# Loads whose source runs span several partitions: 48 KB reads for 12 KB and 24 KB destination rows

## The chip, the cores and the metric

One core of a Trainium2 chip, the others idle. The metric is device time in microseconds of one execution. The rounds of the experiments ran on three chips (0, 12 and 3 in the record), each with the kernel before beside them; hence its medians of 261.81, 262.06 and 262.07 us. "Ratio" is the mean time of one kernel's fast runs over that of the kernel before in the same rounds, with a 95% interval, so it is not quite the ratio of the medians that stand beside it.

## The reference

```python
batch, m, k, n = 16, 512, 768, 1024
x: (batch, k, m) float32;  y: (batch, k, n) float32
out = np.einsum('bkm,bkn->bmn', x, y)          # float32, (16, 512, 1024)
```

Per batch 1.57 MB of x and 3.15 MB of y come in, 2.10 MB go out: 109.05 MB in all.

## The kernel before

K is laid over the 128 partitions with six neighbouring k rows each, so that one partition's share of x is one run of 12 KB in HBM (the device memory) and that of y one of 24 KB. The loads go into float32 staging tiles (two of each), are cast to bfloat16 on the vector engine (DVE), multiplied, copied from PSUM (where matmul results arrive) by the scalar engine, and stored four batches late. All transfers are issued by the sync engine (SP) on one queue.

```python
x_v = x.rearrange("b (p ko) m -> b p ko m", ko=KT)      # KT = 6
y_v = y.rearrange("b (p ko) n -> b p ko n", ko=KT)
o_v = out.rearrange("b (p mo) n -> b p mo n", mo=MT)    # MT = 4
...
for b in range(B):
    xs = xs_pool.tile([P, KT, M], FP32, name="xs")      # bufs=2
    ys = ys_pool.tile([P, KT, N], FP32, name="ys")      # bufs=2
    nc.sync.dma_start(xs[:], x_v[b])
    nc.sync.dma_start(ys[:], y_v[b])
    if b >= LAG:                                        # LAG = 4
        store(b - LAG)
    ...
    nc.vector.tensor_copy(x_sb[:], xs[:])
    for h in range(2):
        ks = slice(h * KT // 2, (h + 1) * KT // 2)
        nc.vector.tensor_copy(y_sb[:, ks], ys[:, ks])
    ...   # 48 matmuls, 8 evictions
for b in sorted(o_tiles):
    store(b)
```

## Time and profile before

| | before |
|---|---|
| median time | 261.97 us (261.96 to 262.15, 3 runs) |
| span in the profile | 260.1 us |
| busiest compute engine | PE 74% |
| packets in flight on the load and store queue | 98.5% of 16 engines' span |
| period of two batches | 31.63 us |

Read it as follows. A busy share of 74% is no bound; the queue's share is. The two staging buffers make the chain repeat every two batches, so the distance between a y cast and the one two batches later is the pace of the steady state. I take it throughout as the mean of the four last periods, from the y cast of batch 7 to that of batch 15: (235.12 - 108.59) / 4 = 31.63 us. From the chain in order of time (start, duration, what):

```profile
108.59 3.44 DVE y_sb L65 x2
...
235.12 1.76 DVE y_sb L65
```

### The profile page before, as it was taken

To read this page: it belongs to the slowest core of one execution; us is meant where nothing else is said; L and a number is where in the kernel's file an instruction comes from. 1 tells how busy PE (TensorE), PEld (TensorE's weight loads), DVE (VectorE), ACT (ScalarE), POOL (GpSimd) and SP (SyncE) were. 2 spreads that over 40 slices of the span, in tenths; PEclk is the share of its full clock that TensorE was granted. 3 is DMA by queue.
4 is the path that set the end of the run, shared out by engine and by line. 5 is a ranking of instruction groups with operands and counts; after the bars stand their busy time and mean duration, and the time that the engine had idled before them with its cause. 6 is when DMAs were issued, how large, how long until landed. Compare 5 with 4: busy or idle time off the path is not lost.

```text
span 260.1 us, 1877 instructions
## 1 busy us (share of the span) xinstructions
PE 192.3 (74%) x768; PEld 89.3 (34%) x768; DVE 83.0 (32%) x48; ACT 76.4 (29%) x129; POOL 0.2 (0%) x4
## 2 busy tenths in 40 slices
PE   0059999896947939599597886939779395895950
PEld 0014555353523514235143342514334142351420
DVE  0271643525213252222524215252132522225000
ACT  1003444342421403314123241413324042141330
POOL 0000000000000000000000000000000000000000
PEclk9999999999997998959779797997999899796895
DMA  7999999999999999999999999999999999999995
GB/s 299 427 423 420 438 433 427 431 369 422 430 430 432 432 430 435 430 432 423 433 435 421 438 422 438 429 427 437 435 424 424 432 431 430 437 425 432 431 408 242
DMA packets 6921, 109.18 MB, mean 420 GB/s; under 512 B 768, under 2 KB 768, under 8 KB 768
## 3 DMA queue, kind: packets, MB, share of 16 engines
q1 hardware_dynamic: 6912, 109.05, 98.5%
q8 instruction: 6, 0.10, 0.1%
q14 instruction: 3, 0.02, 0.0%
HBM read 75.50 MB, written 33.55 MB: 419 GB/s over the span
## 4 chain that ended last, share of the span: by engine, by line
DMA 80%; DVE 10%; PE 5%; DVEq 1%; SPq 0%; issue 0%; ACT 0%
DMA ys<-in_y_dram 80%; DVE y_sb L65 10%; PE ps L74 5%; DVEq L106 1%; SPq L56 0%; ACT o_sb L76 0%; SPq L57 0%; DVEq L65 0%
## 5 line engine op out<-in xcount | busy, mean ns | idle before, releaser
L74 PE MATMUL ps<-y_sb,x_sb 128*128 128x512 bf16 x768 | 192.3, 413 | 58.4 <-DVE y_sb L65 58.4
L74 PEld LDWEIGHTS <-x_sb 128*128 128x128 bf16 x768 | 89.3, 118 | 160.9 <-issue 47.5
L76 ACT COPY o_sb<-ps 128x512 f32<-128x512 f32 x128 | 75.2, 587 | 174.1 <-PE ps L74 174.1
L65 DVE CAST y_sb<-ys 128x3072 bf16<-128x3072 f32 x32 | 54.9, 1757 | 89.4 <-DMA ys<-in_y_dram 89.4
L62 DVE CAST x_sb<-xs 128x3072 bf16<-128x3072 f32 x16 | 28.2, 1760 | 66.2 <-DMA xs<-in_x_dram 55.2
L76 ACT ACT_TABLE_LOAD x1 | 1.3, 1283 | 0.7 <-PEq L95 0.7
L95 POOL MEMSET const-uint8-127<- 128x1 uint8 x1 | 0.1, 103 | 0.0
L95 POOL MEMSET const-bfloat16-1.0<- 128x1 bf16 x1 | 0.1, 102 | 0.0
L95 POOL MEMSET const-float32-1.0<- 128x1 f32 x1 | 0.1, 100 | 0.0
L95 POOL MEMSET const-float32-0.0<- 128x1 f32 x1 | 0.1, 99 | 0.2 <-issue 0.2
## 6 DMA issues: line engine op xcount, KB each, us to landing
ys<-in_y_dram SPq DMA_DIRECT2D x16, 3072.0 KB, 28.1
out_dram<-o_sb SPq DMA_DIRECT2D x16, 2048.0 KB, 32.6
xs<-in_x_dram SPq DMA_DIRECT2D x16, 1536.0 KB, 29.7
```

Source lines behind the costliest of these rows:

```text
L62: nc.vector.tensor_copy(x_sb[:], xs[:])
L65: nc.vector.tensor_copy(y_sb[:, ks], ys[:, ks])
L74: nc.tensor.matmul(ps[:], x_w[:, kt, mo], y_sb[:, kt, ns], start=(kt == 0), stop=(kt == KT - 1))
L76: nc.scalar.copy(o_sb[:, mo, ns], ps[:])
L95: nc = _bacc.Bacc("TRN2", target_bir_lowering=False, num_devices=1)
L106: with _tile.TileContext(nc) as tc:
```

## The change

The intent, from the packet records that the prediction reads: a transfer shows 144 packets (6912 for 48 transfers), and their median times leave about 8 ns a packet at zero bytes. If one read covers four partitions' rows of x, or two of y, there are fewer reads, of 48 KB. The destination keeps one row per partition, 12 KB of x and 24 KB of y.

```diff
+    def load(dst, src, rows):
+        like = template.ins
+        pat = mybir.BassSymbolicTensorAccessPattern
         ...
+        wide = src.rearrange("(q r) k m -> q (r k m)", r=rows)
+        flat = dst.rearrange("p k m -> p (k m)")
+        nc.sync.add_instruction(_copy.replace(
+            like, name=nc.get_next_instruction_name(),
+            ins=(pat(ap=wide.ap, dtype=wide.dtype, bass_ap=wide, **copy_args),),
+            outs=(pat(ap=flat.ap, dtype=flat.dtype, bass_ap=flat, **copy_args),),
+            ant_dge_precooked=False))
...
-            nc.sync.dma_start(xs[:], x_v[b])
-            nc.sync.dma_start(ys[:], y_v[b])
+            if b == 0:
+                template = nc.sync.dma_start(xs[:], x_v[b])
+                nc.sync.dma_start(ys[:], y_v[b])
+            else:
+                load(xs[:], x_v[b], 4)
+                load(ys[:], y_v[b], 2)
```

The rest of the diff (a matmul helper, a loop over a single half) issues the same instructions in the same order.

More of the change, by code (lines that the diff above doesn't have):

```diff
@@ L3 @@
 _os.environ.setdefault("NEURON_RT_ULTRASERVER_MODE", "4")
+import copy as _copy
 from contextlib import ExitStack
@@ L45, with mm @@
     LAG = 4
+    KH = KT // 2
     o_tiles = {}
+    copy_args = dict(is_dma=False)
+    def load(dst, src, rows):
+        like = template.ins
+        pat = mybir.BassSymbolicTensorAccessPattern
+        n = src.shape[1] * src.shape[2]
+        wide = src.rearrange("(q r) k m -> q (r k m)", r=rows)
[5 more added lines that the diff above has]
+            ant_dge_precooked=False))
     def store(b):
         nc.sync.dma_start(o_v[b], o_tiles.pop(b)[:])
+    def mm(ps, x_w, y_sb, kt, mo, nt):
+        nc.tensor.matmul(ps[:], x_w[:, kt, mo], y_sb[:, kt, nt * NF:(nt + 1) * NF],
+                         start=(kt == 0), stop=(kt == KT - 1))
     with tc.manual_schedule():
@@ L55 @@
             ys = ys_pool.tile([P, KT, N], FP32, name="ys")
-            nc.sync.dma_start(xs[:], x_v[b])
-            nc.sync.dma_start(ys[:], y_v[b])
+            halves = 1
+            if b == 0:
[4 more added lines that the diff above has]
+                load(ys[:], y_v[b], 2)
             if b >= LAG:
@@ L63 @@
             for h in range(2):
-                ks = slice(h * KT // 2, (h + 1) * KT // 2)
+                ks = slice(h * KH, (h + 1) * KH)
                 nc.vector.tensor_copy(y_sb[:, ks], ys[:, ks])
@@ L68 @@
             o_tiles[b] = o_sb
-            for mo in range(MT):
-                for nt in range(NT):
-                    ns = slice(nt * NF, (nt + 1) * NF)
-                    ps = psum.tile([P, NF], FP32, name="ps")
-                    for kt in range(KT):
-                        nc.tensor.matmul(ps[:], x_w[:, kt, mo], y_sb[:, kt, ns],
-                                         start=(kt == 0), stop=(kt == KT - 1))
-                    nc.scalar.copy(o_sb[:, mo, ns], ps[:])
-            if False:
-                store(b)
+            ps = {}
+            for h in range(halves):
+                for mo in range(MT):
+                    for nt in range(NT):
+                        if h == 0:
+                            ps[mo, nt] = psum.tile([P, NF], FP32, name="ps")
+                        for kt in range(h * KT // halves, (h + 1) * KT // halves):
+                            mm(ps[mo, nt], x_w, y_sb, kt, mo, nt)
+                        if h == halves - 1:
+                            nc.scalar.copy(o_sb[:, mo, nt * NF:(nt + 1) * NF], ps[mo, nt][:])
         for b in sorted(o_tiles):
```

## The prediction

Where the text below marks a cut, it had named rules and mechanisms that no trace or run of this case shows. No term of its sum is among them: 262.0 us less 0.8 to 1.2 us came to 261.2 us, as it stands. The 0.06 that it gives to "over 2% slower" rested nearly all on a rival that is cut with them, about how a transfer is spread over the engines; take it as the author's estimate.

> **What bounds the kernel now.** I read the page first (busy shares, slices, queue table, issues), then the chain in order of time, the groups by tile, the queue's own timeline, and stretches of the end.
>
> Busy shares, the DMA rows of the slices and the queue table, from the page:
>
> ```profile
> PE 192.3 (74%) x768; PEld 89.3 (34%) x768; DVE 83.0 (32%) x48; ACT 76.4 (29%) x129; POOL 0.2 (0%) x4
> ...
> DMA  7999999999999999999999999999999999999995
> GB/s 299 427 423 420 438 433 427 431 369 422 430 430 432 432 430 435 430 432 423 433 435 421 438 422 438 429 427 437 435 424 424 432 431 430 437 425 432 431 408 242
> DMA packets 6921, 109.18 MB, mean 420 GB/s; under 512 B 768, under 2 KB 768, under 8 KB 768
> ...
> q1 hardware_dynamic: 6912, 109.05, 98.5%
> ```
>
> No compute engine passes 74%. The one hardware queue has packets in flight for 98.5% of 16 engines' span, and only the two end slices, the last but one and one near 55 us fall below 420 GB/s. The count shows how transfers are cut today: 6912 / 48 transfers = 144 packets each, 128 rows and 16 small ones (48 x 16 = the 768 under 512 B). So a packet is one partition's row: 12 KB of x, 24 KB of y, 16 KB of output.
>
> The issues, then the start of the two last links of the chain in order of time:
>
> ```profile
> ys<-in_y_dram SPq DMA_DIRECT2D x16, 3072.0 KB, 28.1
> out_dram<-o_sb SPq DMA_DIRECT2D x16, 2048.0 KB, 32.6
> xs<-in_x_dram SPq DMA_DIRECT2D x16, 1536.0 KB, 29.7
> ```
>
> ```profile
> 175.30 28.09 DMA ys<-in_y_dram
> ...
> 203.49 3.44 DVE y_sb L65 x2
> 206.93 0.02 issue
> 206.94 28.08 DMA ys<-in_y_dram
> ...
> 238.60 12.09 PE ps L74 x45
> ```
>
> A y load takes 28.1 us from issue to landing though 3.1 MB need only about 7.3 us of the engines: the rest is other transfers queued ahead of it. The chain's casts only pass on buffers; what it spends 80% of the span on is a queue that never empties. The pace is the queue's: y casts start at 171.85, 203.49 and 235.12 us, 31.63 us for two batches, 13.63 MB, 431 GB/s.
>
> **What one packet costs.** The trace's packet records have three sizes on this queue, 2048 packets of each. Their median times: 12,288 B 460 ns, 16,384 B 611 ns, 24,576 B 912 ns. From first to last the slope is 12,288 B / 452 ns = 27.19 B/ns, times 16 engines 435.0 GB/s; the middle size fits it (8 + 603 = 611). What is left at zero bytes is **8 ns a packet**. A small packet that ends a transfer takes 9 ns. Packets overlap a little: for two batches one engine's records add up to 2 x 8 x (460 + 611 + 912) + 6 x 9 ns = 31.78 us where 31.63 us passed, so each of the 54 records hides about 2.8 ns. A packet's net fixed cost is then 5 to 8 ns.
>
> [...] The trace has an overhead of that nature, 5 to 8 ns; whether it belongs to the read or the write side it can't show, since both have 128 rows now.
> [...]
>
> **The change part by part.**
> 1. Removed: in 15 of 16 batches (batch 0 keeps its loads) x is read in 32 runs of 48 KB in place of 128 of 12 KB, y in 64 runs of 48 KB in place of 128 of 24 KB. For one engine: 8 to 2 reads for x, 8 to 4 for y, so 6 + 4 = 10 fewer a batch, 150 in all. Destination rows stay 8 + 8. Bytes and stores stay the same. If the fixed cost goes with read runs, 150 x 8 = **1.2 us** by the raw intercept, 150 x 5.2 = **0.8 us** by the net one. If it goes with destination rows, 0.
> 2. Added: these 30 loads are built by copying the first load's instruction and are marked as not prepared in advance[...]. Today a load issue takes 0.33 us and a store's 0.42 us; I allow up to 0.8 us. It is off the path: a load lands 28 to 30 us after issue, of which its own transfer is 7.3 us (y) or 3.7 us (x), so about 20 us of other work lies ahead of it. Cost 0.
> 3. Moved: nothing else. The matmul helper, the single half and the copies issue the same 768 matmuls and 128 evictions in the same order. Batch 0 keeps its first 4.7 MB, so the start does not change.
> 4. The end: y of the last batch lands at 235.03 us; 25.1 us follow. Five stores (10.49 MB) are then to be written, 24.1 us at 435 GB/s, beside a compute chain of 3.4 + 12.1 + 0.6 us and a last 2 MB store. Both hang on that landing, so what the loads save reaches the end in full.
>
> Sum: 262.0 - 0.8 to 1.2 if the read side pays, 262.0 if not. I hold the first likelier (about 60%) and predict **261.2 us**.
>
> **The rivals.**
> - *The destination row pays.* The 8 ns is one constant for loads and stores alike, and a store has HBM on its other side, so nothing speaks against it. Then packets may still be recorded differently, but the time stays at 262.0.
> - *A larger gain on the HBM side.* Against it: everything but bytes is small. 109.05 MB at 435.0 GB/s are 250.7 us. Of the 9.4 us of span beyond, about 2 us pass before data flows, and the last two microseconds move almost nothing (16 GB/s from 258 to 259 us, then none). Load packets slower than their median add 128 x (4.8 + 9.4) ns = 1.8 us in all, of which the packet records put 0.4 us in the first 5 us of traffic and 0.9 us near 55 us, where the first store begins. With all load packets' fixed cost (256 x 8 = 2.0 us) gone too, the gain stays under 4 us; 2% is 5.2 us. So a gain of over 2% needs a rate above 435 GB/s, which nothing here shows.
> [...]
> - *The queue starves on longer issues.* Against: it would take an issue some 20 us longer.
> - *Coarser reads even out worse.* A 48 KB run holds an engine for about 1.8 us; if engines drift by a fraction of that at the end, 0.3 to 0.8 us are lost, which would cancel the gain.
>
> **Range and chances.** The middle is 261.2; the low end 260.3 is the full 1.2 us and half a microsecond that I don't foresee. The high end 262.8 holds no gain and a small drift loss. Over 2% faster (under 256.7) 0.02, from the floor above; over 2% slower (above 267.2) 0.06[...]; within 2% 0.92.
>
> **What would show each step.** Read side pays: the packet count falls from 6912 by 15 x (96 + 64) = 2400 to 4512, with 49,152 B packets of about 8 + 1808 = 1816 ns; the queue's share stays near 98.5% and the period of two batches falls from 31.63 by 0.10 to 0.16 us. Destination side pays: the period stays within 0.03 us, whatever the count is. Issue cost hidden: load issues longer than 0.33 us, the middle slices still at or above 430 GB/s. [...] I am wrong if the rate in the middle passes 435 GB/s, if the middle slices fall by more than 1%, or if a gain appears at the start or end rather than in the period.

## The result, and the profile after

The changed kernel took 261.79 us (261.62 to 262.39, 6 runs) beside 261.97 us (261.90 to 262.24, 6 runs) of the kernel before: ratio 0.9996, interval 0.9983 to 1.0009. Five more runs in later rounds gave 261.72 against 262.07 us, ratio 0.9986 (0.9974 to 0.9999).

The DMA rows of the slices and the queue table, from the page of the changed kernel:

```profile
DMA  7998999999999899999999999999999999999995
GB/s 276 439 495 371 476 388 454 431 353 461 411 411 486 368 461 454 416 416 400 469 423 431 451 383 464 411 446 434 401 460 406 464 423 411 456 393 427 423 431 222
DMA packets 4521, 109.18 MB, mean 420 GB/s; under 512 B 768, under 2 KB 768, under 8 KB 768
...
q1 hardware_dynamic: 4512, 109.05, 98.3%
```

The change did to the cutting what it meant to: 4512 packets in place of 6912, exactly 2400 fewer. 1440 of them have 49,152 B, with a commonest time of 1815 ns, a median of 1824 and a mean of 1836 (from the packet records of the trace, which no view of the profile prints). So a packet record follows the read run, not the destination row. The mean rate and the queue's share are as before. The rates of single slices swing more (353 to 495 GB/s between the ends, before 369 to 438); over 110 to 242 us the mean is 429 GB/s, before 430. The swing is one of counting: the row puts all bytes of a packet into the slice in which it starts. With the bytes spread evenly over each packet's record, the slices between the ends hold 391 to 433 GB/s, before 374 to 433 (worked out from the packet records of both traces). The DMA row beside it stays at 8 or 9 tenths between the ends.

The chain in order of time of the changed kernel (start, duration, what):

```profile
108.52 3.44 DVE y_sb L94 x2
...
171.79 3.44 DVE y_sb L94 x2
...
203.43 3.44 DVE y_sb L94 x2
206.87 0.02 issue
206.88 28.07 DMA ys<-in_y_dram
...
235.05 1.76 DVE y_sb L94
```

The pace is (235.05 - 108.52) / 4 = 31.63 us, the same to the hundredth as before, and a y load still takes 28.1 us from issue to landing. 2400 fewer reads changed nothing in the steady state.

The sync engine's timeline, the changed kernel and then the kernel before (start, duration, engine, line, operation):

```profile
111.98 0.47 SPq L81 DMA_DIRECT2D ys<-in_y_dram  x1
112.50 0.58 SPq L67 DMA_DIRECT2D out_dram<-o_sb  x1
```

```profile
112.04 0.33 SPq L57 DMA_DIRECT2D ys<-in_y_dram  x1
112.42 0.42 SPq L50 DMA_DIRECT2D out_dram<-o_sb  x1
```

A load's issue grew from 0.33 to 0.47 us, a store's from 0.42 to 0.58 us, though the stores' source code is the same. In these runs the store's goes with the load issued just before it: with x alone wide, where that load is an ordinary one, a store's issue is 0.42 us again.

### The profile page after: what moved, and what is told of

Its sections match the earlier page's. It is cut to its first block, busy times and chain, and to the rows that moved or that the text cites. A ratio compares the mean times of both kernels' runs of the same rounds, so it can differ in the third digit from the quotient of the medians.

```text
span 260.0 us, 1877 instructions
## 1 busy us (share of the span) xinstructions
PE 193.2 (74%) x768; PEld 89.4 (34%) x768; DVE 83.0 (32%) x48; ACT 76.4 (29%) x129; POOL 0.2 (0%) x4
## 3 DMA queue, kind: packets, MB, share of 16 engines
q1 hardware_dynamic: 4512, 109.05, 98.3%
## 4 chain that ended last, share of the span: by engine, by line
DMA 80%; DVE 10%; PE 4%; DVEq 1%; SPq 1%; issue 0%; ACT 0%
DMA ys<-in_y_dram 80%; DVE y_sb L94 10%; PE ps L70 4%; DVEq L137 1%; SPq L81 0%; ACT o_sb L109 0%; SPq L82 0%; DVEq L94 0%
## 6 DMA issues: line engine op xcount, KB each, us to landing
ys<-in_y_dram SPq DMA_DIRECT2D x16, 3072.0 KB, 28.1
```

## The experiments

Three theories were on the table. **R**: the read run carries a packet's fixed time, and something took the gain back. **W**: the destination piece carries it, and reads cost nothing. **C**: neither does; a plain byte rate holds the queue, and small fixed times are hidden.

### Built by hand, read in single rows

```diff
-                load(xs[:], x_v[b], 4)
-                load(ys[:], y_v[b], 2)
+                load(xs[:], x_v[b], 1)
+                load(ys[:], y_v[b], 1)
```

> Edit: the changed kernel with both row counts set to 1, so every load is built by hand and issued the longer way, but reads 12 KB and 24 KB runs as before. Theory W (the destination row carries the fixed time of a packet, the read run nothing): time equal to before and to the changed kernel, 261.8 to 262.1 us, period of two batches 31.63 us, 6912 packets with medians 460 and 912 ns. Theory R (the read run pays, and the changed kernel lost its gain to the longer issue or another cost of the hand-built loads): 0.8 to 1.2 us slower than before, 262.8 to 263.2. Theory C (a byte rate holds the queue, no fixed time on either side counts): 261.8 to 262.1, as W.

Measured: 261.83 us against 261.81, ratio 0.9999 (0.9983 to 1.0016), 6912 packets, medians 460 and 912 ns. The chain in order of time:

```profile
108.38 3.44 DVE y_sb L94 x2
...
235.00 1.76 DVE y_sb L94
```

Pace (235.00 - 108.38) / 4 = 31.66 us. The issues take 0.47 us (loads) and 0.58 us (stores), as in the changed kernel. The longer issue costs nothing, so it is not what took a gain back. This leaves W, C, or an R whose loss lies in the wide reads themselves.

### Wide for x alone, and for y alone

```diff
-                load(ys[:], y_v[b], 2)
+                nc.sync.dma_start(ys[:], y_v[b])      # x_only_wide
---
-                load(xs[:], x_v[b], 4)
+                nc.sync.dma_start(xs[:], x_v[b])      # y_only_wide
```

> Edit: wide source for x alone (48 KB runs over 4 partitions), y loaded as before. Theory W: time within 0.2 us of before; the 49,152 B packets of x have the fixed times of four destination rows, so a mean near 4 x 460 - 3 x 3 = 1831 to 1840 ns, not 1816. Theory R: x saves 90 packets an engine, 0.4 to 0.7 us, mean packet near 1816 ns, and y's wide loads must then be what takes the gain back. Theory C: within 0.2 us of before, packet mean anywhere from 1815 to 1840.

> Edit: wide source for y alone (48 KB runs over 2 partitions), x loaded as before. Theory W (destination piece pays, the reads nothing): 1.000 of before within 0.2 us, two batches in 31.61 to 31.66 us, packet mean near 2 x 912 less a few ns. Theory R in what is left of it (the read side pays 1 ns or less): at most 60 x 1 ns = 0.06 us, not to be seen. An original Theory R of 5 to 8 ns: 0.3 to 0.5 us faster.

Measured: x alone 262.12 against 261.81 us, ratio 1.0006 (0.9991 to 1.0021), pace 31.61 us, mean of the wide packets 1823 ns. y alone 261.94 against 262.07 us, ratio 0.9994 (0.9981 to 1.0008), pace 31.77 us, mean of the wide packets 1839 ns. That pace misses the 31.61 to 31.66 us which W had asked for: one step, from the cast of batch 7 to that of batch 8, took 16.36 us instead of 15.8, which no run explains; the three periods after it give 31.62 us. Neither half has a gain that the other gives back. The packet means did not do what W asked: 1823 ns for x is below its 1831 to 1840, and y's two rows came out longer than x's four. At so few pieces a packet's recorded time is no measure of the fixed time; why was not shown (in the kernel before, a record overlaps by about 2.8 ns, by the prediction's estimate).

### Destination cut by padding the tiles; then the source cut too

To enlarge the disputed cost, each destination row is broken into six pieces. In the first run the reads stay at 48 KB, in the second they are cut likewise.

```diff
-            xs = xs_pool.tile([P, KT, M], FP32, name="xs")
-            ys = ys_pool.tile([P, KT, N], FP32, name="ys")
+            xs = xs_pool.tile([P, KT, M + 16], FP32, name="xs")[:, :, :M]
+            ys = ys_pool.tile([P, KT, N + 16], FP32, name="ys")[:, :, :N]
...
-        flat = dst.rearrange("p k m -> p (k m)")
+        flat = dst
-        wide = src.rearrange("(q r) k m -> q (r k m)", r=rows)
+        wide = <the same, with a dimension of 1>      # dst_cut
+        wide = src                                    # both_cut
```

> Edit: staging tiles padded by 64 B behind each k row, so a destination row falls into six pieces of 2 KB (x) or 4 KB (y), while the source stays in 48 KB runs. 80 more destination pieces an engine and batch, 1200 in 15 batches, reads as in the changed kernel. Theory W with 4.5 to 8 ns a piece: 5.4 to 9.6 us slower than the changed kernel, 267 to 271 us, packet count still near 4512 plus batch 0's. Theory R: no change, 261.5 to 262.3 us. Theory C: no change, 261.5 to 262.5 us.

> Edit: the padded tiles again, and the source cut likewise into 2 KB and 4 KB runs at the same addresses in the same order: one read for one written piece. 1200 more reads and 1200 more written pieces an engine than the kernel before. Theory W: the same time as the run with only the destination cut, within 0.3 us. Theory R: 5.4 to 9.6 us slower than that run (which is then at 262). If both sides pay: slower than that run by the read side's share. Theory C: still 262, within 0.5 us.

Measured: 270.80 us (ratio 1.0328, 1.0299 to 1.0358) and 269.94 us (1.0304, 1.0289 to 1.0320) against 261.81. R and C, which asked for 262 in the first run, fall if the slowdown is the pieces'. But the run had a second difference, which I had not foreseen. The chain in order of time of the run with the destination alone cut:

```profile
111.60 6.62 DVE y_sb L94 x2
...
242.08 3.35 DVE y_sb L94
```

The pair of y casts takes 6.62 us instead of 3.44 now that they read padded rows (with as many pieces but no padding, next section, it is 3.44 us again). The pace is (242.08 - 111.60) / 4 = 32.62 us with the destination cut, 32.69 us with both. W had asked for 0.3 us at most between the two times; they lie 0.86 us apart, the four times of the first spread over 1.7 us (269.43 to 271.14), and its profile is of the fastest. The verdict needed a version with the old casts.

### Six adjacent pieces, same tiles, same addresses

```diff
-        wide = src.rearrange("(q r) k m -> q (r k m)", r=rows)
-        flat = dst.rearrange("p k m -> p (k m)")
+        wide = src.rearrange("(q r) k m -> q (r k m)", r=rows).rearrange("q (o f) -> q o f", o=1)  # dst6_flat
+        wide = src.rearrange("p k m -> p (k m)").rearrange("p (c f) -> p c f", c=6)                # both6_flat
+        flat = dst.rearrange("p k m -> p (k m)").rearrange("p (c f) -> p c f", c=6)                # both runs
```

> The padded run also doubled the time of the casts (3.43 to 6.62 us for y), so its slowdown could be theirs. Edit: tiles and casts as in the changed kernel, source in 48 KB runs; only the destination pattern names each row as six adjacent pieces of 2 KB (x) or 4 KB (y), no gap between them. Theory W (destination piece pays, 6.2 ns net from the padded run: its two batches took 32.62 us in place of 31.63 with 160 more pieces an engine): two batches in 32.6 us, total 261.8 + 1200 x 6.2 ns = 269.2 us, casts at 1757 ns. Rival: the casts were the cause, or adjacent pieces are joined by the hardware: 261.5 to 262.3 us. Theory R: the same, 262.

> Edit: as the run with six adjacent destination pieces, but the source named in the same six pieces a row, so 80 more reads an engine and batch than with 48 KB runs beside the same writes. Theory W: within 0.5 us of that run (269 us), two batches in 32.6 us, though the packet count rises by some 21,600. If reads pay too, even 2 ns each: 1350 x 2 = 2.7 us more than that run. Rival of joined pieces: 262.

The page's packet count and the chain in order of time, destination alone cut:

```profile
DMA packets 4521, 109.18 MB, mean 406 GB/s; under 512 B 768, under 2 KB 768, under 8 KB 768
```

```profile
112.09 3.44 DVE y_sb L94 x2
...
243.98 1.76 DVE y_sb L94
```

And both sides cut, its packet count and two y casts of DVE's timeline:

```profile
DMA packets 26121, 109.18 MB, mean 406 GB/s; under 512 B 768, under 2 KB 768, under 8 KB 23808
```

```profile
112.18 3.43 DVE L94 CAST y_sb<-ys 128x3072 bf16<-128x3072 f32 x2 [5.82 <-DMA ys<-in_y_dram]
...
244.12 3.43 DVE L94 CAST y_sb<-ys 128x3072 bf16<-128x3072 f32 x2 [5.81 <-DMA ys<-in_y_dram]
```

The casts are back at 3.44 us and the time is 270.83 us (ratio 1.0337, 1.0321 to 1.0352) and 271.04 us (1.0343, 1.0327 to 1.0358) against 262.06. The first kernel has the same 4512 packets on the queue as the changed kernel, the second 26,112, and the paces are 32.97 and 32.99 us. So 160 more destination pieces an engine in two batches cost 32.97 - 31.63 = 1.34 us, **8.4 ns a piece**. 180 more reads an engine in two batches beside them cost 32.99 - 32.97 = 0.02 us, **0.1 ns a read**, which is nothing against the scatter of the pace; the whole times give 0.21 us / 1350 = 0.16 ns. (The expectation's "80 more reads" should be 90; its 1350 is right.) The written pieces themselves are in no count, as a packet is counted by its read; that the pattern makes six of a row is taken from the time. The mean of a 48 KB packet rose from 1836 to 1940 ns, 104 ns for 13.3 more pieces (80 over the six wide packets of an engine and batch), 7.8 ns each: the destination's pieces lengthen a packet that is counted by its read.

### Twelve adjacent pieces

```diff
-        ... c=6 ...
+        ... c=12 ...
```

> Edit: destination rows named as twelve adjacent pieces of 1 KB (x) and 2 KB (y), source in 48 KB runs: 176 more pieces an engine and batch than the changed kernel, 2640 in all. Theory W with a fixed time per piece: 2.2 times the rise of the six-piece run: 2640 x 6.2 ns = 16.4 us, 278 us, two batches in 33.8 us. A rival in which small pieces cost by their size and not by their number, or a read side that hides part, gives no such proportion. Theory R: 262.

> Edit: source and destination both named in twelve adjacent pieces. Theory W: within 1 us of the run with twelve destination pieces and 48 KB reads, 278 us; 2790 more reads an engine cost nothing. If each read cost 0.5 ns: 1.4 us more. Theory R: 262 plus 2790 x 5 to 8 ns over the run with wide reads, that is 14 us or more above it.

Measured: 283.21 us (ratio 1.0808, 1.0790 to 1.0826) and 283.52 us (1.0820, 1.0804 to 1.0837). Two y casts of DVE's timeline, destination alone cut:

```profile
118.06 3.43 DVE L94 CAST y_sb<-ys 128x3072 bf16<-128x3072 f32 x2 [6.20 <-DMA ys<-in_y_dram]
...
256.61 3.43 DVE L94 CAST y_sb<-ys 128x3072 bf16<-128x3072 f32 x2 [6.13 <-DMA ys<-in_y_dram]
```

Pace (256.61 - 118.06) / 4 = 34.64 us. With both sides cut:

```profile
118.32 3.43 DVE L94 CAST y_sb<-ys 128x3072 bf16<-128x3072 f32 x2 [6.21 <-DMA ys<-in_y_dram]
...
256.73 3.43 DVE L94 CAST y_sb<-ys 128x3072 bf16<-128x3072 f32 x2 [6.15 <-DMA ys<-in_y_dram]
```

Pace 34.60 us. Against the kernel before, 352 more pieces cost 3.01 us, 8.6 ns each; against six pieces, 192 more cost 1.67 us, 8.7 ns each. The rise is a straight line from the uncut kernel on, and that ends C: had the uncut kernel been held by a byte rate with room to spare, the first pieces would have been cheaper than the later ones. 372 more reads an engine in two batches cost nothing in the pace (34.60 against 34.64 us) and 0.31 us / 2790 = 0.11 ns each in the whole time.

My expectation of 269.2 and 278 us was too low, since I took 6.2 ns from the padded run. Why a padded piece costs 6.2 ns in the pace and an adjacent one 8.4 is open (the profiled padded run was the fastest of four, which can be a part of it). Also open is why the whole time gives less than the pace: (270.83 - 262.06) us / 1200 = 7.3 ns, (283.21 - 262.06) us / 2640 = 8.0 ns. In these runs an issue of a load or store often takes 3 to 11 us, the longest 13.7 us. So another rival is that the issuing, and not the engine's work on a piece, sets the pace. The twelve-piece run with wide reads, sync engine and then DVE:

```profile
109.28 7.14 SPq L81 DMA_DIRECT2D ys<-in_y_dram  x1
116.47 9.28 SPq L67 DMA_DIRECT2D out_dram<-o_sb  x1
```

```profile
135.50 3.43 DVE L94 CAST y_sb<-ys 128x3072 bf16<-128x3072 f32 x2 [6.29 <-DMA ys<-in_y_dram]
```

The issue of this y load ends at 116.42 us, its data is awaited until 135.50 us: 19 us lie between, more than the transfer itself needs (four wide packets an engine, about 8.3 us by the mean below). The queue doesn't run dry either, its DMA share from 110 to 242 us is 1.00 to 1.05 in the four runs with adjacent pieces (1.01 in the kernel before), and the wide packets themselves grew, to a mean of 2076 ns (240 ns for 29.3 pieces, 8.2 ns each). All this speaks against issuing as the limit; why the issues are long was not shown.

### The changed kernel again

> The changed kernel itself, five rounds, for a narrower interval. Theory W: ratio 1.000, within 0.1 us of before. Theory R as predicted (0.8 to 1.2 us): ratio 0.9954 to 0.9970. If the interval excludes 0.9970, the predicted gain is excluded by time alone.

Ratio 0.9986, interval 0.9974 to 0.9999. The predicted gain of 0.8 to 1.2 us (0.9970 or less) is excluded by time alone, in these rounds and in the first ones. The pace was 31.62 us. By the medians it was 0.35 us faster, more than the 0.1 us that W allowed. A gain of some tenths of a microsecond is compatible with both intervals (0.9983 to 0.9999); the first of them holds 1 and the runs do not settle whether there is one; in the pace there is none.

### The last store in two halves, on the kernel before

I saw no way to make the loads' destination rows longer, as a partition's row of a batch is all there is (a load of two batches at once was not tried). So the one other loss in sight was tried, the uneven end.

```diff
+        for b in sorted(o_tiles):
+            if b < B - 1:
+                store(b)
+        for mo in range(0, MT, 2):
+            nc.sync.dma_start(o_v[B - 1][:, mo:mo + 2], o_tiles[B - 1][:, mo:mo + 2])
```

> A look for what a store's timing at the end is worth, on the kernel before: the last batch's 2 MB store is issued as two halves, the first after the first four evictions. The stretch from 250 to 258 us moved 2.97 MB, which at 435 GB/s needs 6.8 us, so at most 1.2 us are to be had; 8 more destination pieces an engine cost 8 x 8.4 ns = 0.07 us. Expected 0.4 to 1.0 us faster, ratio 0.996 to 0.9985. If the end hangs on the engines' uneven finishing and not on the late issue: no change.

Measured: 262.22 against 262.07 us, ratio 1.0000 (0.9987 to 1.0012): my expectation failed. Stretches of the end, the kernel before and then this run (columns: stretch, length, busy time and count of each engine, clock, DMA share, GB/s):

```profile
251.00:252.00 1.00, 0.00 (x0) 0.00 (x0) 0.00 (x0) 0.29 (x1) 0.00 (x0) 1.00 0.66 279
```

```profile
251.00:252.00 1.00, 0.00 (x0) 0.00 (x0) 0.00 (x0) 0.00 (x0) 0.00 (x0) 1.00 0.94 401
...
256.00:257.00 1.00, 0.00 (x0) 0.00 (x0) 0.00 (x0) 0.00 (x0) 0.00 (x0) 0.50 0.66 279
257.00:258.00 1.00, 0.00 (x0) 0.00 (x0) 0.00 (x0) 0.00 (x0) 0.00 (x0) 0.50 0.33 139
```

The dip at 251 us is gone (0.94 in place of the 0.66 of the kernel before), but the last y cast came 0.28 us later in this profile (235.40 us), and the final microseconds empty as slowly as before (from 256 to 259 us 279, 139 and 49 GB/s, in the kernel before 328, 180 and 16). What the filled dip gained was lost before or after it; with one profile of each I can't say which. No version beats both kernels clearly.

## Why the prediction was right, and where it was not

**The bound** was read rightly: pace, rate and queue share are those of before, and the issues and the matmuls changed nothing. Its own signs for the middle slices ("at or above 430 GB/s", wrong "if the middle slices fall by more than 1%") fail slice by slice, as single slices swing from 353 to 495; they hold only for the mean from 110 to 242 us, 429 against 430 GB/s. The sign that it set for the destination side came: the period stayed within 0.03 us.

**Part 1, the step that failed.** "If the fixed cost goes with read runs, 150 x 8 = 1.2 us ..., 150 x 5.2 = 0.8 us ... I hold the first likelier (about 60%)". The runs put the cost on the other branch, "if it goes with destination rows, 0": 8.4 to 8.7 ns for a destination piece, 0.2 ns or less for a read run at 1350 and 2790 more of them, as long as reads are not more numerous than written pieces (see below). The size of the fixed time, 8 ns before overlap, was near; its place was not. (The pieces measured have 1 to 4 KB; what a whole row of 12 or 24 KB has was not measured apart.) 261.2 us was thereby 0.5 to 0.6 us low (measured 261.79 and 261.72). It lies inside the range because the range had left room for the zero branch; with both branches inside it, the hit says nothing for the branch that was chosen. The trace of the kernel before could not decide it, as the prediction said itself: both sides had 128 rows. The prediction gives no reason for leaning to the read side. The sign that it set for that side, the packet count, came to the last packet (4512), with a commonest time of 1815 ns as worked out (1816), and it meant nothing for the time.

**Part 2.** The issue did grow, by 0.14 us (0.33 to 0.47), less than the 0.8 us allowed, and lies off the path: the run with hand-built single-row loads has a ratio of 0.9999.

**Parts 3 and 4.** No instruction moved; from the last y cast to the end of the span it is 260.0 - 235.05 = 25.0 us, as before.

**The rivals.** *The destination row pays*: shown, within the limit below. *A larger gain on the HBM side*: the ratio's lower limit of 0.9974 leaves no 2%. *A loss from the way the 32 or 64 reads are spread over the engines*: no such loss, as the pace is 31.63 us and the mean rate 429 GB/s, before 430; each load still has 16 small packets (768 for 48 transfers, as before). *The queue starves*: no, and in the runs with cut rows not even with issues of 3 to 11 us (DMA share 1.00 to 1.05 from 110 to 242 us). *Coarser reads even out worse*: not seen apart; wide packets' mean is 21 ns above their commonest time, but the pace does not show it.

One limit stays. The cost of reads was tested where each read is as large as its written piece or larger; a load whose reads are smaller than the piece they fill did not compile, so no run has one. So the runs show that the destination's number of pieces sets the fixed time as long as reads are not more numerous. Whether a read side with more pieces than the write side would pay is open: "the more numerous side pays" fits every run here as well as "the destination pays".

## What to carry to other kernels

Before merging descriptors, ask which side of the transfer carries the fixed time, and test it by cutting one side finer: a cost that is too small to be seen when removed is plain when it is multiplied (8.4 ns a destination piece became 8.8 us with 1200 more pieces an engine). A packet count that falls by a third is no gain in itself (6912 to 4512 here, ratio 0.9996); take the steady-state period as the judge, look at its single steps for a late batch, and know that here a packet was counted by its read (4512, with the destination whole or in six) and lengthened by its writes (1836 to 1940 ns). In the loads of this kernel the contiguous row per partition is what counted, as long as reads are not more numerous than written pieces: cutting the rows from 12 and 24 KB to 2 and 4 KB cost 3.4%, to 1 and 2 KB 8.1%; joining reads over partitions bought nothing with rows of 12 and 24 KB (ratios 0.9996 and 0.9986) and made a load's issue 0.14 us longer.
